# A row softmax whose loads are issued by Pool and whose stores are issued by SP, instead of SP and ACT

## The chip, the cores and the metric

The kernel runs on one core of one Trainium2 chip; the other cores are idle. The metric is the device time of one execution in microseconds (us), as the median of several runs, lower being better. The engines are called by the names of the profile: DVE is the vector engine, ACT the scalar engine, POOL (or Pool) is GpSimd, SP is the sync engine. A transfer between the chip's memory and the on-chip SBUF is issued by one of SP, ACT and Pool, but the bytes are moved by the core's 16 DMA engines, whoever issued it. A transfer is cut into pieces, each told by a descriptor (here mostly one of 32 KB for each partition); the profile counts each piece as a packet. It calls the queues of SP and ACT "hardware_dynamic" and that of Pool "software_dynamic". I call the latter the software path; on it Pool has to write the descriptors itself, as the prediction says from its source.

## The reference

```python
x = randn(32, 512, 1024), float32;  temperature = 0.5

scaled  = x / temperature
shifted = scaled - max(scaled, axis=-1)
exp_x   = exp(shifted)
return exp_x / sum(exp_x, axis=-1)
```

There are 16384 rows of 1024 numbers. The kernel must read 67.11 MB and write 67.11 MB.

## The kernel before

The rows are cut into 16 tiles of 4 MB. Each tile has 128 partitions, with 8 whole rows (32 KB, contiguous in memory) in each. Six data buffers hold tiles. A tile is loaded into a buffer, worked on in place in two groups of 4 rows in each partition, and stored from the same buffer; the next load into that buffer waits until the store has landed. What the change and the argument touch is this (cuts are marked with "..."):

```python
TILES = [[8]] * 16
BUFS = 6
GROUP = 4
...
    def load():
        i = len(tiles)
        if i < len(TILES):
            xt = data.tile([P, sum(TILES[i]), d], f32, name="xt")
            nc.sync.dma_start(out=xt, in_=dram(xf, i))          # L61, issued by SP
            tiles.append(xt)

    def maximum(g):       # DVE: row maxima of a group, then bias = -scale * max
        ...
    def exponential(g):   # ACT: exp(scale * x + bias) in place, row sums on the side
        ...
    def divide(g):        # DVE
        nc.vector.reciprocal(recip, sums)
        for b in range(k):
            nc.vector.tensor_scalar_mul(                        # L93
                tiles[i][:, a + b, :], in0=tiles[i][:, a + b, :], scalar1=recip[:, b : b + 1])

    def store(g):
        ...
            nc.scalar.dma_start(out=dram(of, i)[:, a : a + k, :],
                                in_=tiles[i][:, a : a + k, :])  # L101, issued by ACT
            if a + k == sum(TILES[i]):
                load()

        for _ in range(BUFS):
            load()
        for g in range(len(groups) + 1):
            if g < len(groups):
                maximum(g)
                exponential(g)
            if g > 0:
                divide(g - 1)
                store(g - 1)
```

Note one thing for later: on DVE the maximum of group g comes before the divide of group g - 1.

## Time and profile before

| | before |
|---|---|
| median time | 318.1 us |
| span of the profiled run | 316.0 us |
| bytes moved | 134.25 MB, 425 GB/s over the span |
| DVE / ACT / POOL busy | 75% / 47% / 0% |

These lines are from the profile's page of the kernel before. The row "DMA" cuts the span into 40 equal slices and gives in each the busy share of the 16 DMA engines in tenths; the lines q1 (SP's queue) and q10 (ACT's queue) give packets, MB and the share of the DMA engines' time; the L70 line is the reduction for the maximum with its busy time, the mean ns of one, and the idle time of DVE before it; the last two give the us from issue to landing.

```profile
DMA  8999999999999999999999999999999999999996
q1 hardware_dynamic: 2304, 67.11, 49.7%
q10 hardware_dynamic: 2304, 67.11, 49.2%
L70 DVE TENSOR_REDUCE top<-xt 128x4 f32<-128x4096 f32 x32 | 141.3, 4416 | 62.6 <-DMA xt<-in_x_dram 62.6
xt<-in_x_dram SPq DMA_DIRECT2D x16, 4096.0 KB, 50.2
out_dram<-xt ACTq DMA_DIRECT2D x16, 4096.0 KB, 38.6
```

The table of windows of the kernel before has, for each stretch, its length, the busy time of DVE, ACT and POOL, the granted clock, the busy share of the DMA engines, and GB/s.

```profile
0.00:20.00 20.00, 7.00 (x3) 3.66 (x6) 0.20 (x4) 1.00 0.95 393
20.00:80.00 60.00, 59.27 (x57) 39.25 (x68) 0.00 (x0) 1.00 1.00 427
80.00:280.00 200.00, 151.57 (x147) 97.39 (x168) 0.00 (x0) 1.00 1.00 433
280.00:303.00 23.00, 17.65 (x19) 9.27 (x16) 0.00 (x0) 1.00 1.00 433
```

Read together: the DMA engines are full from 20 us to 303 us and move 427 to 433 GB/s. The two queues get equal shares. No compute engine is the limit; DVE idles 62.6 us waiting for loads. A load lands 50 us after its issue, while a tile takes about 19.4 us, so 50.2 / 19.4 = 2.6 loads are on their way at any time. By the same numbers a load is issued with some 30 us of earlier loads in front of it (50.2 less 19.4, an estimate).

The chain of waits shows one such issue in the kernel before (start, length, what): a store lands, SP issues the load that was waiting for the buffer after 0.02 + 0.03 us, and the load lands 49.92 us later.

```profile
77.00 38.52 DMA out_dram<-xt
115.52 0.02 SPq L61
115.54 0.03 issue
115.57 49.92 DMA xt<-in_x_dram
```

### The profile page before, as it was taken

The numbers are of one execution on the slowest core, as the hardware profiler recorded it, in microseconds if no ns is written. First come the engines' busy times: TensorE is split into PE (matmuls) and PEld (weight loads), VectorE is DVE, ScalarE is ACT, GpSimd is POOL, SyncE is SP. The second block draws the span as 40 slices with busy tenths as digits, with TensorE's granted clock in tenths as the row PEclk, the third lists the DMA queues.
The fourth block names the chain that finished last, engine by engine and source line by source line (L and its number), as shares of the span: only waits on it lengthen the run. The fifth ranks groups of instructions, "written<-read, shape, count | busy, mean of one in ns | idle before, by whom it ended". The sixth has DMA issues, their size and how long they took to land.

```text
span 316.0 us, 620 instructions
## 1 busy us (share of the span) xinstructions
DVE 235.5 (75%) x224; ACT 149.6 (47%) x257; POOL 0.2 (0%) x4
## 2 busy tenths in 40 slices
DVE  0399999999689494994949859497693976949720
ACT  0176666666526255361554605546064560645500
POOL 0000000000000000000000000000000000000000
DMA  8999999999999999999999999999999999999996
GB/s 332 411 452 423 373 460 415 452 425 431 436 427 440 427 444 423 444 419 448 415 452 411 452 408 456 423 444 427 436 431 432 440 423 444 419 444 419 452 411 274
DMA packets 4612, 134.25 MB, mean 425 GB/s; under 512 B 512, under 2 KB 512, under 8 KB 512
## 3 DMA queue, kind: packets, MB, share of 16 engines
q1 hardware_dynamic: 2304, 67.11, 49.7%
q10 hardware_dynamic: 2304, 67.11, 49.2%
q14 instruction: 4, 0.03, 0.0%
HBM read 67.11 MB, written 67.11 MB: 425 GB/s over the span
## 4 chain that ended last, share of the span: by engine, by line
DVE 49%; DMA 32%; another core or an unknown queue 9%; ACT 5%; issue 1%; DVEq 0%; SPq 0%
DVE top L70 29%; DMA xt<-in_x_dram 20%; DVE xt L93 18%; DMA out_dram<-xt 12%; ACT xt L79 5%; DVE recip L91 1%; DVE bias L73 1%; DVEq L147 0%; SPq L61 0%
## 5 line engine op out<-in xcount | busy, mean ns | idle before, releaser
L79 ACT ACTIVATE xt<-xt,bias 128x1024 f32<-128x1024 f32 x128 | 145.4, 1137 | 136.8 <-DVE recip L91 119.4
L70 DVE TENSOR_REDUCE top<-xt 128x4 f32<-128x4096 f32 x32 | 141.3, 4416 | 62.6 <-DMA xt<-in_x_dram 62.6
L93 DVE TENSOR_SCALAR xt<-xt,recip 128x1024 f32<-128x1024 f32 x128 | 87.7, 749 | 1.1
L79 ACT ACTIVATION_READ_ACCUMULATOR xt<-xt,bias 128x1 f32 x128 | 23.9, 187 | 0.0
L79 ACT ACT_TABLE_LOAD x1 | 1.3, 1283 | 13.0 <-DMA xt<-in_x_dram 13.0
L91 DVE RECIPROCAL recip<-sums 128x4 f32<-128x4 f32 x32 | 5.5, 171 | 2.1 <-ACT xt L79 2.1
L73 DVE TENSOR_SCALAR bias<-top 128x4 f32<-128x4 f32 x32 | 5.4, 170 | 1.1
L133 POOL MEMSET const-bfloat16-1.0<- 128x1 bf16 x1 | 0.1, 101 | 0.0
L133 POOL MEMSET const-uint8-127<- 128x1 uint8 x1 | 0.1, 101 | 0.0
L133 POOL MEMSET const-float32-0.0<- 128x1 f32 x1 | 0.1, 98 | 0.2 <-issue 0.2
L133 POOL MEMSET const-float32-1.0<- 128x1 f32 x1 | 0.1, 98 | 0.0
## 6 DMA issues: line engine op xcount, KB each, us to landing
xt<-in_x_dram SPq DMA_DIRECT2D x16, 4096.0 KB, 50.2
out_dram<-xt ACTq DMA_DIRECT2D x16, 4096.0 KB, 38.6
```

The source lines that it names most:

```text
L70: nc.vector.tensor_reduce(out=top, in_=tiles[i][:, a : a + k, :], axis=mybir.AxisListType.X, op=extreme)
L73: nc.vector.tensor_scalar_mul(bias, in0=top, scalar1=-scale)
L79: nc.scalar.activation(tiles[i][:, a + b, :], tiles[i][:, a + b, :], mybir.ActivationFunctionType.Exp, bias=bias[:, b : b + 1], scale=scal ...
L91: nc.vector.reciprocal(recip, sums)
L93: nc.vector.tensor_scalar_mul(tiles[i][:, a + b, :], in0=tiles[i][:, a + b, :], scalar1=recip[:, b : b + 1])
L133: nc = _bacc.Bacc("TRN2", target_bir_lowering=False, num_devices=1)
```

## The change

The intent is to free ACT, which computes the exponentials, from issuing transfers, and to give loads and stores an issuer each that does nothing else. The whole diff:

```diff
-            nc.sync.dma_start(out=xt, in_=dram(xf, i))
+            nc.gpsimd.dma_start(out=xt, in_=dram(xf, i))
 ...
-            nc.scalar.dma_start(out=dram(of, i)[:, a : a + k, :], in_=tiles[i][:, a : a + k, :])
+            nc.sync.dma_start(out=dram(of, i)[:, a : a + k, :], in_=tiles[i][:, a : a + k, :])
```

The instructions of DVE and their order do not change. ACT loses 16 issues, Pool gains 16.

## The prediction

> **What bounds the kernel now.** The transfers. The page says 134.25 MB at a mean of 425 GB/s over a span of 316.0 us, and its row of 40 slices has the DMA at 9 everywhere but in the first and last slice. In the table of windows DMA share is 1.00 in every window from 20 to 303 us, at 427 to 434 GB/s; 134.25 MB at 433 GB/s is already 310 us. The other 6 us are the start (first load issued at 0.73 us, landing 12.2 us later) and the tail (last store issued at 302.38 us, about 13 us of store). No engine is the bound: DVE is 75% busy, ACT 47%. From 84 us on DVE waits about 4.5 us per 19.4 us tile for a load (62.6 us in total in the groups).
>
> **What the change moves.** The order of instructions on DVE is unchanged; ACT loses its 16 issues (0.34 us each, 5.4 us), which it can spare: it waits 119.4 us for DVE. No store gets earlier: in the timeline ACT issues a store at the moment the divide ends (divide ends 62.19, issue 62.22). So ACT's relief is worth 0.
>
> Loads now need descriptors written by GpSimd. The Trainium skill ("DMA: Bandwidth & Descriptors", Latency and other measured facts) gives about 1 us to the first byte on that path against 0.6 us; only the first load is exposed, so I estimate +0.5 to +1.5 us at the start. Later loads have slack: issue to landing is 50 us in the trace, while a tile takes 19.4 us, so about 2.6 loads are in flight and one issued 10 us late would still arrive in time.
>
> The skill ("SBUF — State Buffer", SBUF: two separate sides) warns that a two-port VectorE operation locks GpSimd out while it writes descriptors. The divide runs at 749 ns for 1024 elements a partition, against 4414 ns for 4096 in the reduction, so it is faster than one element per 0.96 GHz cycle and probably such an operation; four in a row last 2.74 us. That bounds each delay at about 3 us, once per load and hidden by the 30 us of queue. The first six loads are issued while DVE is idle.
>
> What can matter is the sharing of the 16 DMA engines between the two queues. Now both use equal packets (2304 each for 67.11 MB, 49.7% and 49.2% of the time). I expect that to stay. If the software queue got the smaller share, the last load would land later; it now lands at 282.6 us, and the work behind it (19.8 us of compute, then the store) leaves the DMA with just enough stores. Stores served strictly first would, I estimate, leave it idle for some 10 us near the end. Loads served first would cost nothing.
>
> **Prediction.** 319 us, range 316.5 to 324; faster by over 2%: 0.02, within 2%: 0.90, slower by over 2%: 0.08.
>
> **What would show it.** DMA share 1.00 and about 433 GB/s in the middle windows; the first reduction starts at 13.5 to 14.5 us instead of 12.96; the load queue is of a software kind with about 2304 packets and half of the DMA time; DVE's wait for loads stays near 60 us; the last store is issued 20 us after the last load lands.
>
> **What would make it wrong.** Smaller packets or slower engines on the software path, seen as under 425 GB/s in the middle windows; an unequal sharing of the queues with an idle DMA between last load and last store; descriptor writing held up so long that the load queue runs dry, seen as DMA share below 1.00 with DVE waits growing; a long first start of GpSimd's software.

## The result, and the profile after

The changed kernel takes 318.86 us (318.64 to 319.19, 4 runs) against 318.08 us (318.0 to 318.13, 4 runs). The ratio is 1.0026, with a 95% interval of 1.0008 to 1.0043: a real loss, but a quarter of a per cent. All ratios here are the mean time of one kernel's runs over that of the other's of the same rounds, so they are not quite the ratios of the medians.

The same lines of the page, for the changed kernel (q0 is now Pool's queue, q1 is SP's):

```profile
DMA  6999999999999999999999999999999999999996
q0 software_dynamic: 2304, 67.11, 49.5%
q1 hardware_dynamic: 2304, 67.11, 49.0%
L70 DVE TENSOR_REDUCE top<-xt 128x4 f32<-128x4096 f32 x32 | 141.3, 4416 | 63.6 <-DMA xt<-in_x_dram 63.6
xt<-in_x_dram POOLq DMA_DIRECT2D x16, 4096.0 KB, 49.4
out_dram<-xt SPq DMA_DIRECT2D x16, 4096.0 KB, 38.8
```

And the same windows:

```profile
0.00:20.00 20.00, 5.64 (x3) 2.30 (x2) 3.48 (x10) 1.00 0.88 365
20.00:80.00 60.00, 59.26 (x57) 40.42 (x71) 1.06 (x2) 1.00 1.01 428
80.00:280.00 200.00, 152.95 (x147) 96.46 (x169) 4.24 (x8) 1.00 1.00 432
280.00:303.00 23.00, 17.20 (x19) 10.38 (x18) 0.00 (x0) 1.00 1.00 433
```

The two profiles differ in rate in one window, the first: 365 instead of 393 GB/s over 20 us, which is 0.56 MB, or 1.3 us at 433 GB/s. In the others the rates agree within 1 GB/s, and the events are only shifted. The first reduction starts at 14.33 us instead of 12.96 us, that of the last tile (which starts as its load lands) at 283.72 us instead of 282.62 us, the last store is issued at 303.48 us instead of 302.38 us, and the span is 317.2 us instead of 316.0 us.

The chain of the changed kernel has the counterpart of the store and load shown before:

```profile
96.75 39.24 DMA out_dram<-xt
136.06 0.50 issue
136.56 49.36 DMA xt<-in_x_dram
```

The store lands at 135.99 us and Pool's instruction starts at 136.56 us: 0.57 us, of which the trace calls 0.50 us "issue", where SP needed 0.05 us. So a load is issued later on the software path. It costs nothing here, because, as I read it, the load still spends 49 us in flight behind earlier loads. The experiments test this reading.

### The profile page after: what moved, and what is told of

It reads as the page before. It is cut to its first block, busy times and chain, and to the rows that moved or that the text cites. A ratio compares the mean times of both kernels' runs of the same rounds, so it can differ in the third digit from the quotient of the medians.

```text
span 317.2 us, 639 instructions
## 1 busy us (share of the span) xinstructions
DVE 235.5 (74%) x224; ACT 149.6 (47%) x257; POOL 8.8 (3%) x20
## 3 DMA queue, kind: packets, MB, share of 16 engines
q0 software_dynamic: 2304, 67.11, 49.5%
q1 hardware_dynamic: 2304, 67.11, 49.0%
## 4 chain that ended last, share of the span: by engine, by line
DMA 60%; DVE 30%; ACT 3%; another core or an unknown queue 1%; issue 1%; DVEq 0%; POOLq 0%; ACTq 0%; PEldq 0%
DMA xt<-in_x_dram 35%; DMA out_dram<-xt 25%; DVE top L70 18%; DVE xt L93 11%; ACT xt L79 3%; DVE bias L73 1%; DVE recip L91 0%; DVEq L147 0%; ACTq L147 0%; POOLq L61 0%; POOLq L147 0%; PEldq L147 0%
## 5 line engine op out<-in xcount | busy, mean ns | idle before, releaser
L61 POOL DMA_DIRECT2D xt<-in_x_dram x16 | 8.6, 538 | 225.5 <-DMA out_dram<-xt 205.5
```

Of the source, the lines that this page charges most:

```text
L61: nc.gpsimd.dma_start(out=xt, in_=dram(xf, i))
```

## The experiments

Theory A: the software path makes every load land about 1 us later; all of these but the first are hidden behind the loads already queued, so the cost is one delay at the start. Theory B: the software path costs a little throughout, through its descriptors or a slower DMA. A further question of the prediction was whether DVE's divide holds up Pool's writing of descriptors, and another whether the sharing of the queues could have mattered.

### The changed kernel again, on the chip of the next three runs

> The changed kernel once more, beside its variants on one chip. Both theories: about 318.9 us, 0.2 to 0.3% above the kernel before; first reduction at about 14.3 us.

Measured: 318.82 us (318.61 to 319.22, 5 runs) against 318.07 us (9 runs), ratio 1.0023 (1.0009 to 1.0036). The first reduction starts at 13.93 us this time. The delay at the start is thus 1.0 to 1.4 us in two profiles, and the loss in time is 0.75 us. That the loss is less than the delay comes back below, with the stores.

### The first six loads back to SP

```diff
-            nc.gpsimd.dma_start(out=xt, in_=dram(xf, i))
+            (nc.sync if i < BUFS else nc.gpsimd).dma_start(out=xt, in_=dram(xf, i))
```

> The changed kernel, but the six loads at the start are issued by SP; the ten later ones stay with Pool. Theory A (the whole cost is the later landing of the first load, everything after it is hidden in the load queue): time of the kernel before, 318.1 us, ratio 1.000 within 0.1%; first reduction at about 13.0 us, last load landing at about 282.6 us. Theory B (the software path costs a little on each load, or its descriptors slow the DMA engines in the steady state): the ten later loads keep 10/16 or more of the cost, so 318.6 us or more, ratio 1.0015 or more.

Measured: 317.60 us (317.46 to 317.9), ratio 0.9986 (0.9973 to 0.9998). With ten of sixteen loads still issued by Pool, nothing of the loss is left. The first reduction starts at 13.21 us. This is theory A; theory B, which wanted a ratio of 1.0015 or more, is out. The kernel is even 0.5 us faster than the one before, just outside the 0.1% that theory A allowed.

One expectation failed: the last load was to land at about 282.6 us, but the last tile's reduction starts at 271.59 us, and the last store is issued at 291.34 us instead of 302.38 us. Loads now stand in two queues, one of them shared with the stores, so the engines' turns probably fall otherwise. DVE has less left to do between 280 and 303 us (9.30 us instead of 17.65 us), yet the DMA engines are as full, at the same rate:

```profile
280.00:303.00 23.00, 9.30 (x12) 5.57 (x10) 0.00 (x0) 1.00 1.00 433
```

So loads and stores that are issued 11 us earlier did not make the kernel 11 us faster: here the DMA engines were busy throughout from 20 to 303 us, and the order of transfers hardly counted. This also means that the run changes more than the issuer of the first loads, and I have no shown cause for the 0.5 us.

### Only the first six loads to Pool

This is the mirror image: the kernel before, with only the start on Pool.

```diff
-            nc.sync.dma_start(out=xt, in_=dram(xf, i))
+            (nc.gpsimd if i < BUFS else nc.sync).dma_start(out=xt, in_=dram(xf, i))
```

> The kernel before, but the six loads at the start are issued by Pool; the ten later ones stay with SP, the stores with ACT. Theory A: the whole cost is here, about 318.9 us, ratio 1.0025; first reduction at about 14.3 us. Theory B: at most 6/16 of the cost, about 318.4 us, ratio 1.001.

Measured: 319.11 us (318.94 to 320.05), ratio 1.0037 (1.0024 to 1.005). The whole loss is there, as theory A has it. The first reduction starts at 13.80 us. The order moves as in the run before (the last tile's reduction starts at 270.12 us), and again the total does not follow it. Both runs move the six first loads together; that the first of them alone costs time is inferred from the queue, not tested.

### Pool's loads, with the stores left on ACT

```diff
-            nc.sync.dma_start(out=xt, in_=dram(xf, i))
+            nc.gpsimd.dma_start(out=xt, in_=dram(xf, i))
```

> Only the loads move to Pool; ACT keeps the stores. If moving the stores from ACT to SP is worth nothing, as predicted: same as the changed kernel, 318.9 us, store issues within 0.1 us of the end of the divide. If SP's freedom had hidden a part of the software path's cost: over 319.5 us. If the move had cost: below 318.5 us.

Measured: 319.39 us (318.72 to 319.88), ratio 1.0037 (1.0024 to 1.005), where the full change had 1.0023 (1.0009 to 1.0036). The intervals overlap, and the last store is issued at 303.36 us in this run's profile and at 303.48 and 303.37 us in the two of the changed kernel. So this run alone cannot say whether moving the stores from ACT to SP was worth anything. But the two pairs of runs with the same start agree: with a start on Pool, 319.39 us with stores on ACT and 318.82 us with stores on SP; with a start on SP, 318.07 us (the kernel before) and 317.60 us. In both the kernel with its stores on SP is faster by about 0.5 us. With a start on Pool costing about 1.2 us (ratios of 1.0037), this would give the 0.75 us of the whole change. It is not shown, as in the second pair the later loads differ too; the run that would settle it, the kernel before with only its stores on SP, was not made.

### Two buffers instead of six

If six buffers hide the later landing of each load, two buffers must show it. The rival here is that only Pool's first issue is late. Both kernels keep their stores on ACT, so that only the issuer of the loads differs.

```diff
-BUFS = 6
+BUFS = 2
```

> The kernel before with 2 data buffers instead of 6, so that no second load waits in the queue. One buffer goes through load (about 12 us alone, more beside a store), compute of about 20 us and store (12.8 us): estimated 43 us or more for two tiles, 350 to 390 us in all, DMA share well under 1. This is the base of the next run.

> The same two-buffer kernel with the loads issued by Pool (the stores stay with ACT). Theory A (six buffers hide a later landing of about 0.9 to 1.4 us of every load): now each load's delay is on the path, once per pair of tiles, 8 times 0.9 to 1.4 us, so 7 to 11 us more than the two-buffer kernel with SP loads (2 to 3%). Rival (the software path's later landing is a one-time cost of Pool's first issue): under 2 us more.

Measured: 494.58 us (494.25 to 494.78) with SP and 506.46 us (505.81 to 506.67) with Pool, 11.9 us more. The direction is theory A's, and the rival, which allowed under 2 us more, is out. But both expectations missed: 494.6 us instead of 350 to 390 us, and 11.9 us of difference instead of 7 to 11 us. The chains show why. These are one tile of the two-buffer kernel with SP loads:

```profile
126.58 11.10 DMA out_dram<-xt
137.69 0.02 SPq L61
137.71 0.03 issue
137.74 12.15 DMA xt<-in_x_dram
149.91 4.43 DVE top L70
...
154.63 2.80 ACT xt L79 x5
157.43 11.10 DMA out_dram<-xt
```

And one tile of the same kernel with Pool loads:

```profile
129.70 11.14 DMA out_dram<-xt
...
140.86 0.04 POOLq L61
140.90 0.50 issue
141.41 12.48 DMA xt<-in_x_dram
153.91 4.43 DVE top L70
...
158.62 2.80 ACT xt L79 x5
161.43 11.11 DMA out_dram<-xt
```

The chain goes through every tile, not through every second one: the store of a tile waits for a divide which stands behind the next tile's first reduction on DVE, and that waits for the next load. (The 2.80 us piece called "ACT" runs beside that divide.) So load, reduction, divide and store follow one another with no overlap, 30.8 us a tile with SP and 31.7 us with Pool. I had expected the two tiles to overlap, hence the 350 to 390 us, and the delay to count once per pair of tiles, hence the 7 to 11 us.

From one store's issue to the next is 157.43 - 126.58 = 30.85 us with SP and 161.43 - 129.70 = 31.73 us with Pool, 0.88 us more. About 0.5 us of this is the longer time from the store's landing to the start of Pool's instruction (0.57 us instead of 0.06 us); 0.3 to 0.4 us is a later landing after that (12.48 instead of 12.15 us here, medians 12.5 and 12.2 us). Fourteen loads wait for a buffer, and 14 times 0.88 us is 12.3 us, against 11.9 us measured. This is what one load through Pool costs when somebody waits for it. The six-buffer kernel starts with the same delay: Pool's first instruction starts at 1.24 us, SP's at 0.73 us, 0.51 us later, as for each load here.

### Does the divide hold up Pool?

In the changed kernel none of Pool's ten later issues falls into a divide: all ten start during a reduction, and each takes 0.53 us. So the trace of the change says nothing about the lock that the prediction discussed, in which the divide keeps Pool from writing descriptors until it ends. I cut each load into 8 loads of 16 partitions, to have 128 issues spread over time.

```diff
-            nc.gpsimd.dma_start(out=xt, in_=dram(xf, i))
+            for q in range(8):
+                nc.gpsimd.dma_start(
+                    out=xt[16 * q : 16 * (q + 1)], in_=dram(xf, i)[16 * q : 16 * (q + 1)]
+                )
```

> The changed kernel with each load cut into 8 loads of 16 partitions, so that Pool issues 128 times, many of them while DVE is in the divide (in the changed kernel all ten later issues fall into a reduction or just after a divide). If the divide locks Pool out while it writes descriptors: issues that begin in a divide last up to 0.75 us longer each (or up to 2.7 us if four divides in a row hold the lock), or the divide lasts longer beside an issue; issues within a reduction keep one short duration, about 0.5 us. If there is no lock: all issues have the same duration, and the divide stays at 745 to 755 ns. Time: within 2% of the kernel before either way; the shorter load queue may cost some us.

Of the issues after the first eight, 24 begin while a divide runs, and 22 of these take 0.55 to 1.05 us. The other 96 issues, many of them within a reduction, all take 0.49 us. The timeline of this run shows one of each kind (start, length, engine, line, instruction):

```profile
232.75 4.41 DVE L73 TENSOR_REDUCE top<-xt 128x4 f32<-128x4096 f32 x1
235.94 0.49 POOL L62 DMA_DIRECT2D xt<-in_x_dram  x1 [1.73 <-DMA xt<-in_x_dram]
237.49 2.74 DVE L96 TENSOR_SCALAR xt<-xt,recip 128x1024 f32<-128x1024 f32 x4
238.65 1.01 POOL L62 DMA_DIRECT2D xt<-in_x_dram  x1 [2.21 <-DMA xt<-in_x_dram]
```

So the hold-up exists, but is at most 1.05 - 0.49 = 0.56 us. It never lasts through the four instructions of a divide (2.74 us): the largest added time is shorter than one of them (0.75 us). The ends say where Pool gets in: each of the 22 ends 94 to 98 ns after one of the four instructions ends, mostly with more of the divide to come (for the one above, at 239.66 us, with the divide running to 240.23 us).

The time was not within 2%, as I had expected, but 528.29 and 537.24 us in two runs (the longer one, which was profiled, is over 1.5% above the other; I use it for the lengths of Pool's instructions and not for its time). The next run looks into this. Two runs are too few for more than the size of this loss.

### The same cut with SP as the issuer

> A control for the run with loads in 8 on Pool, which took 532.8 us with the DMA at only 118 GB/s in its first 100 us: the same cut, but loads from SP and stores from ACT as in the kernel before. If the slow rate comes from the shape[...]: again about 118 GB/s at the start and a time over 450 us. If it comes from Pool's path: about 330 GB/s or more at the start and a time under 360 us.

Measured: 743.83 us (740.73 to 746.93, 2 runs), ratio 2.34. The first 40 us of the run with Pool and of the run with SP, as the table of windows has them, in this order:

```profile
0.00:40.00 40.00, 0.00 (x0) 0.00 (x0) 7.58 (x19) 1.00 1.01 118
```

```profile
0.00:40.00 40.00, 0.70 (x1) 0.74 (x1) 0.20 (x4) 1.00 1.00 118
```

The rate is 118 GB/s with either issuer, at a DMA share of 1.00. So the rate at the start comes from the shape and not from Pool's path. The Trainium skill ("SBUF — State Buffer", Door 1: The DMA port swizzle) says that DMA bandwidth depends on how many of 16 ports the partitions reach, and by its table 16 consecutive partitions reach 4 of them; a quarter of its 435 GB/s is an estimate of 109 GB/s, near the 118 GB/s measured. Why SP is slower still over the whole run is not shown. SP waited 501.7 us for stores before its loads, and from 100 to 300 us the engines moved 189 GB/s, against 266 GB/s with Pool; but the stores are on ACT in this run and on SP in the other, and I did not separate the two.

### The same cut with a divide that is no two-port operation

The skill ("SBUF — State Buffer", Who interferes with whom) says that a multiplication by a per-partition scalar can run in a two-port mode which locks GpSimd out, while a two-input operation has no such mode and takes only the read side. So I made the divide a two-input multiplication, on Pool's 8-part loads.

```diff
-            nc.vector.tensor_scalar_mul(
-                tiles[i][:, a + b, :], in0=tiles[i][:, a + b, :], scalar1=recip[:, b : b + 1]
-            )
+            nc.vector.tensor_tensor(
+                out=tiles[i][:, a + b, :], in0=tiles[i][:, a + b, :],
+                in1=recip[:, b : b + 1].to_broadcast([P, d]), op=mybir.AluOpType.mult)
```

> The run with loads in 8 on Pool, but DVE divides by a two-input multiplication (the reciprocal broadcast as the second input), [...]about 1.1 us instead of 0.75 us. If it is the two-port mode of the divide that holds up Pool: all of Pool's issues now last 0.49 us, also those that begin in a divide. If any DVE instruction that writes a whole row holds it up: issues that begin in a divide last 0.55 to 1.6 us. Time about as that run, 525 to 550 us.

Measured: 553.87 us (550.43 to 557.31), at the upper end of the expectation or above it. The divide takes 1.22 us a row instead of 0.75 us. Now 35 issues begin while a divide runs, and all 35 take 0.49 us. One of them in the timeline:

```profile
267.10 4.63 DVE L96 TENSOR_TENSOR xt<-xt,recip 128x1024 f32<-128x1024 f32 x4
267.40 0.49 POOL L62 DMA_DIRECT2D xt<-in_x_dram  x1 [4.39 <-DVE recip L94]
```

It is the fast form of the divide that holds up Pool, and not any DVE instruction that writes a whole row. The runs agree with the skill here.

### Unequal sharing of the two queues

The prediction held that the change could have cost some 10 us if the loads had got the smaller share of the DMA engines. I gave the loads smaller descriptors, once on Pool and once on SP in the kernel before.

```diff
-            nc.gpsimd.dma_start(out=xt, in_=dram(xf, i))
+            nc.gpsimd.dma_start(out=xt, in_=dram(xf, i), max_dma_last_dim=4096)
```

> The changed kernel, but the loads are cut into descriptors of 4 KB instead of 32 KB; the stores keep 32 KB. If the DMA engines take one descriptor from each queue in turn, the loads get about one ninth of the engines while a store is waiting: stores land in 10 to 14 us instead of 39, loads land much later, the last load lands later than 283.7 us, and the DMA idles between last load and last store: estimated 324 to 330 us, DMA share under 0.8 in the last 30 us. If Pool's path packs descriptors into larger packets so that the queues still share equally: within 1% of the changed kernel, load and store landing near 49 and 39 us. Either way shows whether the queue shares that the prediction worried about can cost anything.

> The kernel before with the same 4 KB descriptors for its SP loads. If sharing is by descriptor on the hardware path: as in the run with Pool's 4 KB loads, 324 to 330 us, with stores landing in 10 to 14 us and DMA idle near the end. If not: 318 to 320 us. A difference between this run and the one with Pool loads shows how the two paths cut transfers into packets.

Measured: 338.04 us (337.78 to 338.48) with Pool, ratio 1.0629, and 336.78 us (336.66 to 336.89) with SP, ratio 1.0588. The difference of the two, 1.3 us, is again about the cost of Pool's start. These are lines of the page and of the windows of the SP run:

```profile
q1 hardware_dynamic: 16640, 67.11, 50.0%
q10 hardware_dynamic: 2304, 67.11, 46.5%
out_dram<-xt ACTq DMA_DIRECT2D x16, 4096.0 KB, 15.4
240.00:280.00 40.00, 29.08 (x29) 18.31 (x31) 0.00 (x0) 1.00 0.99 412
300.00:312.00 12.00, 8.81 (x8) 4.18 (x7) 0.00 (x0) 1.00 0.21 86
```

A store now lands in 15.4 us instead of 38.6 us, and so it does with Pool's loads (15.4 us as well). The last tile's reduction starts at 303.12 us instead of 282.62 us, and between 300 and 312 us, while the last tile is computed, the DMA engines are busy for only 21% of the time: 12 us times 0.79 is 9.5 us idle. That is the loss which the prediction estimated at some 10 us. The total loss was larger, 18.8 us of span, because the rate fell as well. By the windows (412 to 429 GB/s) the run moved 118.1 MB between 20 and 300 us, 422 GB/s, which at 433 GB/s would have taken 7.3 us less. I had not expected that part, hence my 324 to 330 us. Some 2 us of the 18.8 us are in neither.

I expected loads of small descriptors to get one ninth of the engines beside a store, and so they did. One store of the SP run is issued at 150.91 us. In the middle of it, from 155 to 163 us, the two queues moved as many packets each:

```profile
q10 hardware_dynamic: 96, 3.15, 91.0%
q1 hardware_dynamic: 96, 0.39, 11.9%
```

The loads thus moved 0.39 of 3.54 MB, 11%, with pieces of 4 KB against 32 KB. With Pool's loads the counts are 96 for the loads and 99 for the stores in a like stretch (156 to 165 us). The Trainium skill ("DMA: Bandwidth & Descriptors", Queues, rings and completion order) says that each DMA engine takes turns between queues packet by packet. The runs agree, where the packets are those that the profile counts: the queue with the larger pieces gets more, in the proportion of 8 to 1. That the store still needs 15.4 us, and not the 10 to 14 us expected, is due to its beginning: from 151 to 154.3 us only packets of loads move. What holds up the store for that time stays open.

For the change itself this closes the point: with equal descriptors Pool's queue and the hardware queue share equally (49.5% and 49.0%), and with unequal ones Pool's queue fares as SP's does.

## Why the prediction was right

The predicted time was 319 us, within 316.5 to 324; the measured one is 318.86 us.

1. *The transfers bound the kernel.* Right. The middle windows stay at a DMA share of 1.00 to 1.01 and 427 to 433 GB/s in both kernels. Issuing the last store 11 us earlier, as in the run with the first six loads on SP, went with a gain of only 0.5 us.
2. *ACT's relief is worth 0.* Right to within about 0.5 us. Leaving the stores on ACT changed the ratio from 1.0023 to 1.0037, with overlapping intervals, and the last store leaves 19.8 us after the last load lands, as before. Two pairs of runs hint at a gain of about 0.5 us from the stores on SP. If it is real, the nearness of 318.86 to 319 is in part luck.
3. *Only the first load's delay is exposed, 0.5 to 1.5 us.* Right. The first reduction starts 1.37 us later in one profile and 0.97 us later in the repeat, the span is 1.2 us longer, the median 0.8 us. Putting the first six loads back on SP removed the loss; putting only those six on Pool produced it. That it is the first of the six is inferred.
4. *Later loads have slack.* Right. Without the slack, in the two-buffer kernel, the same delay costs 11.9 us.
5. *The cost of a Pool load.* The skill ("DMA: Bandwidth & Descriptors", Latency and other measured facts) gives about 1 us to the first byte instead of 0.6 us, a difference of 0.4 us. Here the difference was 0.88 us a load. After the instruction's start it was 0.3 to 0.4 us, which agrees; the other 0.5 us come before Pool's instruction shows in the profile at all. The prediction's range covered this, but its source alone would have given too little.
6. *Each hold-up by the divide is bounded at about 3 us.* True as a bound, but too large by a factor of five: it is at most 0.56 us, as the lock does not last through four instructions. In the changed kernel it does not occur, because the ten later issues all fall into a reduction. Why they do was not tested; each waits for a store to land.
7. *The queues share equally.* Right: 2304 packets each, 49.5% and 49.0%. And the fear behind it was justified in kind: where the stores got the larger share, 9.5 us of idle DMA appear near the end. Where the loads came early (the last tile's reduction at 271.59 and 270.12 us), nothing was lost, as it also said.

## What to carry to other kernels

Who issues a transfer matters only where somebody waits for that issue: count how many transfers are queued ahead of it. With 2.6 loads in flight, 0.88 us more on each load cost about 1 us in the whole kernel; with none in flight they cost 11.9 us. If Pool must issue, give the first loads to a hardware queue, and keep the descriptors of loads and stores of equal size, because the size of the pieces, and not the kind of the queue, decided who got the DMA engines.

## What the Trainium skill lacked or had wrong

- "DMA: Bandwidth & Descriptors", Latency and other measured facts: it gives a first byte after about 1 us on the software path and 0.6 us on the hardware path. Measured here for a 4 MB load: 0.88 us more from the landing of the store that the load waited for to the landing of the load, of which about 0.5 us come before Pool's instruction starts in the profile and 0.3 to 0.4 us after it. The page's difference of 0.4 us fits the second part only.
- "SBUF — State Buffer", SBUF: two separate sides: it says that the lock is held for the whole instruction, and warns of starvation, without saying what a row of such instructions does. Here four of them back to back (2.74 us) delayed Pool by at most 0.56 us, in 22 of the 24 issues that began among them, and each of these ended within 0.1 us of the end of one of the four.
- "DMA: Bandwidth & Descriptors", Queues, rings and completion order: turns between queues go by packet, which the runs bear out (96 packets of 4 KB against 96 of 32 KB). It gives no hint of what else was seen: a store issued behind such loads moved nothing for over 3 us.
- No page has the time that Pool takes to write the descriptors of one load as a function of their number: the median of Pool's instruction was 487 ns for 16 descriptors of 32 KB, 530 ns for 128, and 873 ns for 1024 of 4 KB. Both steps give an estimate of 0.38 ns for each further one. None of the 16 issues of 1024 began in a divide.
- "Perfetto Trace Analysis", DMA Instruction — SWDGE (GPSIMD): it says that there is no start marker for such an instruction. The traces here give each one a start and a length (487 to 1049 ns in the run with 8-part loads), which is what made the hold-up visible. How the profiler comes by the start is not known here.
